# Dilated queries per head with zero rows, value matmuls with the values moving, differential inputs by head pairs

## The chip, the cores and the metric

The kernel runs on one core of a Trainium2 chip. The metric is device time in microseconds (us) from the program's start to its end. The instruction engines are TensorE (matmuls and transposes; PE in the rows, its weight loads PEld), VectorE (DVE), ScalarE (ACT), GpSimd (POOL) and SyncE (SP). SP and POOL also start DMA transfers, each from a queue of its own.

## The reference

One layer of a decoder trunk: 512 tokens, width 1024, float32. A normalised input h goes through one projection `h @ w_in` into four branches and four gates; the branches are RWKV-7, dilated attention, differential attention and a convolution. Their 256-wide outputs go through `w_branch`, are weighted by sigmoid gates, summed and sent through `w_out`; a SwiGLU block follows. The change touches the two attention branches:

```python
# dilated: 3 groups (window, dilation) x 4 heads of 64, softmax over 3 groups at the end
s = einsum('brcqhd,brckhd->brchqk', qb, kb) * 64 ** -0.5      # plus ALiBi bias and mask
lse = logsumexp(s); o = einsum('brchqk,brckhd->brcqhd', exp(s - lse), vb)
out = sum(softmax(stack(lses)) * stack(outs))
...
# differential: 4 heads, each with two maps of 32 columns, values of 64
s = einsum('bqhmd,bkhmd->bhmqk', q_blk, k) * 32 ** -0.5       # plus ALiBi bias and mask
pr = softmax(s); att = pr[:, :, 0] - lam * pr[:, :, 1]
o = einsum('bhqk,bkhd->bqhd', att, vf)                        # then RMS norm per head
```

## The kernel before, in words

**Products.** A weight block comes by DMA from SP's queue into one of two raw buffers (`wload`, line 135). ScalarE casts it to a high half in float32r (line 154), VectorE subtracts for the low half (line 157), each in two pieces; high and low halves have two buffers each. A product of `cm_gemm` (line 194) runs 8 contraction blocks of three 128x512 matmuls (`mm3`, line 188). Its result lies in PSUM under the tag g, two buffers. The gate products (`gates`, line 311: g for the gate, p for the branch projection) and the dilated q, k products are what TensorE has beside the attention work.

**Order.** Within an engine the instructions run in the order that a scheduler fixes at build time from priorities and dependencies, so that attention matmuls stand between the gate products. `place` and `PLACE` (line 26) put single steps behind a named product. TensorE, ScalarE and VectorE each keep one such order, and an instruction that waits holds all behind it.

**Differential attention.** `diff_gemm` (553) makes q and k and spills them to DRAM by POOL's queue. `diff_chain` (573) reads `lam` (row_lam), then loads stacks of 96 rows: high, low, high of q against high, high, low of k, so that one matmul does a three-term product. There are 8 stack entries for 4 heads of two maps; per pair of heads six loads of 256 KB and half of the bias df_b (512 KB). All of these lie in tiles of their own for both pairs, and POOL issues both sets one behind the other (lines 593 to 601). Then, per pair hp, query tile t, head and map: the score dfs (TensorE, line 617, width at least 256 columns), bias and row maximum (VectorE, df_x and df_nm, 620), exponential (ScalarE, 622), the two maps joined (VectorE, 628), transposes dfp (631), a copy pT (ScalarE, 633). The value matmul dfo (638) has the values as the stationary operand, 64 columns, and pT as the moving one, 128 columns:

```python
nc.tensor.matmul(out=o[i * 64:i * 64 + 64, tq], lhsT=X["v"][:, j, h * 64:(h + 1) * 64], rhs=PT[i][:, j, :],
                 start=(j == 0), stop=(j == t))
```

so the two heads of a pair write the two 64-row halves of one PSUM tile (tag o). At the end o is copied to z, transposed back (dfr, four per pair, 645), scaled, normed per head (df_m, and df_r with `pow` on POOL, line 227), transposed (dfy) and split into the branch's y.

**Dilated attention.** `dil_product` (694) makes q and k for a pair of heads and a group. Heads lie in the lower and upper 64 rows of a tile. Group 0 is split into high and low halves (`split_from`: ScalarE casts, VectorE subtracts); groups 1 and 2 are copied with their tokens sorted by residue mod 4. In `dil_chain` (720) the scores dls contract over one head's 64 rows: three float32r matmuls of 256 columns for kind 0 (744), two float32 matmuls of 128 columns for kind 1 (747). Then follow bias, exponential, transposes dlp (753), copies, and value matmuls dlo (763), of the same form as dfo. Kind 1's statistics are exchanged by two small DMAs (774, 776), the weights of both kinds are spread over 64 columns (dl_rb), transposed (dlw, 795) and multiplied onto the outputs. Two biases dl_b of 512 KB (716) come by POOL's queue behind gate02's split.

Of the kernel before, what the change touches and what calls it, by code (L numbers as in the profile page):

```python
# [108 lines left out]
def kern(tc, A):  # L109
    nc = tc.nc  # L110
    W = A["wblk"]
    with ExitStack() as ctx:
# [150 lines left out]
        with ExitStack() as mx:  # L263
            mp = mx.enter_context(tc.tile_pool(name="mix", bufs=1, reuse_waits="tile"))
            with ExitStack() as bx:
# [39 lines left out]
                env = dict(hold=hold, behind=behind, place=place, later=later, after_norm=after_norm, products=products, wx=wx, splits=splits, ups=ups, nc=nc, tc=tc, A=A, vec=vec, HALF=HALF, ps=ps, gps=gps, sps=sps, ops=ops, cm_gemm=cm_gemm, tm_gemm=tm_gemm,  # L305
# [266 lines left out]

def diff_chain(E, pool, X):
# [5 lines left out]
    bias = pool.tile([128, 4, S], F32, name="df_b")  # L579
# [109 lines left out]
def dil_tiles(pool, hp):  # L689
    out = {(n, g): pool.tile([128, S], dt, name=f"dl_{n}{g}{hp}") for n, g, dt in DIL_PARTS}  # L690
    return out


def dil_product(E, hp, nm, g, out):

    p = E["gps"](f"dl{nm}{hp}{g}")
    E["cm_gemm"](p, f"dil_{nm}{hp}{g}")
    if g == 0:
        E["split_from"](p, out[(nm + "0", 0)], out[(nm + "1", 0)])
    else:  # L700
        with E["tc"].high_priority(offset=PRI):
            E["nc"].scalar.copy(out=out[(nm, g)].rearrange("p (r i) -> p r i", r=4), in_=p.rearrange("p (i r) -> p r i", r=4))
# [10 lines left out]
def dil_bias(E, pool, hp):  # L713
    bias = pool.tile([128, 2, 512], F32, name=f"dl_b{hp}")
    with E["tc"].issue_after(E["splits"]["gate02"]):
        E["nc"].gpsimd.dma_start(out=bias, in_=E["A"]["dilb"][:, 2 * hp:2 * hp + 2, :])
    return bias


def dil_chain(E, pool, hp, qk, bias, v, y):  # L720
    nc, ident, sps, pps, ops = E["nc"], E["ident"], E["ops"], E["sps"], E["ups"]
    num, st = [], []
    for kind in range(2):
        o = ops([128, S], f"dlo{hp}{kind}")
        stat = pool.tile([128, NT, 2, 2], F32, name=f"dl_st{hp}{kind}", tag=f"dl_st{kind}", bufs=2)
        for t in range(NT):
# [44 lines left out]
        st.append(stat)

    dS = E["dram"].tile([S, 4], F32, name=f"dl_dS{hp}")
    nc.gpsimd.dma_start(out=dS.rearrange("(i r) s -> i r s", r=4), in_=st[1].rearrange("p r h s -> p r (h s)"))
    sB = pool.tile([128, NT, 2, 2], F32, name=f"dl_sB{hp}", tag="dl_sB", bufs=2)
    nc.gpsimd.dma_start(out=sB.rearrange("p t h s -> p t (h s)"), in_=dS.rearrange("(t p) s -> p t s", p=128))
    w = pool.tile([128, 2, NT, 2], F32, name=f"dl_w{hp}", tag="dl_w", bufs=2)
    d = pool.tile([128, 2, NT, 2], F32, name=f"dl_d{hp}", tag="dl_d", bufs=2)
    both = (st[0], sB)
    nc.vector.tensor_tensor(out=d[:, 0], in0=st[0][:, :, :, 0], in1=sB[:, :, :, 0], op=ALU.min)  # L780
    for k in range(2):
        nc.vector.tensor_tensor(out=w[:, k], in0=d[:, 0], in1=both[k][:, :, :, 0], op=ALU.subtract)
    nc.scalar.activation(out=w, in_=w, func=AF.Exp)
    for k in range(2):
        nc.vector.tensor_tensor(out=d[:, k], in0=w[:, k], in1=both[k][:, :, :, 1], op=ALU.mult)
    nc.vector.tensor_tensor(out=d[:, 0], in0=d[:, 0], in1=d[:, 1], op=ALU.add)
    nc.vector.reciprocal(out=d[:, 0], in_=d[:, 0])
    rb = pool.tile([128, 2, NT, 2, 64], F32, name=f"dl_rb{hp}", tag="dl_rb", bufs=1)
    for k in range(2):
        nc.vector.tensor_tensor(out=w[:, k], in0=w[:, k], in1=d[:, 0], op=ALU.mult)  # L790
        nc.vector.tensor_copy(out=rb[:, k], in_=w[:, k].unsqueeze(3).to_broadcast([128, NT, 2, 64]))

        p = pps([128, S], f"dlw{hp}{k}")
        for t in range(NT):
            tr = nc.tensor.transpose(out=p[:, t * 128:(t + 1) * 128], in_=rb[:, k, t].rearrange("p a b -> p (a b)"), identity=ident)
            E["later"].setdefault(f"dlw{hp}{k}", tr.ins)
        nc.vector.tensor_tensor(out=num[k], in0=num[k], in1=p, op=ALU.mult)
    nc.vector.tensor_tensor(out=num[0], in0=num[0], in1=num[1], op=ALU.add)
    E["split_from"](num[0], y[0][:, hp, :], y[1][:, hp, :])
# [498 lines left out]
```

## Time and profile before

| quantity | value |
|---|---|
| runs | 994.23, 995.0, 996.42 us, median 995.0 |
| profiled execution | 999.86 us, span 997.9 us |
| granted TensorE clock, mean | 0.991 of full speed |
| TensorE / its weight loads | 97% / 81% busy |
| VectorE / ScalarE / GpSimd | 51% / 36% / 8% busy |

The profile shows one execution. Windows give the busy time in a stretch of time, with the granted clock as a share of full speed; a timeline gives single instructions with start and length, and in brackets the idle time in front and what ended it. A timeline row joins neighbours of one form (x2, x8); a float32 matmul leaves two records. The forms are written as rows and columns of the array (128\*64 is half the columns, 64\*128 half the rows), then the moving operand. Differential attention lies between 300 and 431 us, the dilated chains between 400 and 473 us.

### The profile page before, as it was taken

How to read it: one execution, taken by the hardware profiler on the slowest of the kernel's cores; microseconds unless marked ns; L12 is line 12 of the kernel's file. 1: busy time of each engine (PE TensorE's matmuls, PEld its weight loads, DVE VectorE, ACT ScalarE, POOL GpSimd, SP SyncE). 2: the span in 40 equal slices, each digit the busy share in tenths (PEclk: the TensorE clock that was granted, in tenths of full speed). 3: DMA queues.
4: the chain of work that ended last, by engine and by line, in shares of the span. 5: the costliest groups of instructions: out<-in, count | busy, mean ns of one | idle time of the engine just before them, and what ended most of it. 6: DMA issues, size and time to landing. Idle time of an engine off the chain costs nothing.

```text
span 997.9 us, 13474 instructions
## 1 busy us (share of the span) xinstructions
PE 971.5 (97%) x5260; PEld 812.9 (81%) x5260; DVE 508.3 (51%) x1098; ACT 361.2 (36%) x746; POOL 77.0 (8%) x119
## 2 busy tenths in 40 slices
PE   6999999999997999999999999999999999999996
PEld 5887888899985777676888899998888888888885
DVE  4899948346443746544556557634333333322224
ACT  5343613221133635535335446533223232321213
POOL 3000230310140000000000001100000000000003
PEclk9999989999998999999999999999999999999999
DMA  5232533301299122121435235332322323223232
GB/s 189 93 110 85 159 108 104 106 22 44 85 188 236 54 74 64 43 64 44 143 107 181 98 105 170 119 115 85 106 93 98 105 85 105 89 101 102 89 106 84
DMA packets 29775, 103.73 MB, mean 104 GB/s; under 512 B 3600, under 2 KB 3792, under 8 KB 29712
## 3 DMA queue, kind: packets, MB, share of 16 engines
q1 hardware_dynamic: 23472, 87.37, 26.5%
q0 software_dynamic: 6096, 15.24, 6.5%
q8 instruction: 41, 0.67, 0.3%
q10 hardware_dynamic: 144, 0.26, 0.1%
q14 instruction: 22, 0.18, 0.1%
HBM read 97.08 MB, written 5.78 MB: 103 GB/s over the span
## 4 chain that ended last, share of the span: by engine, by line
PE 52%; issue 37%; DVE 4%; DMA 4%; POOL 2%; ACT 1%; SPq 0%; DVEq 0%; POOLq 0%; ACTq 0%
PE g L188 17%; PE p L188 4%; PE dlv L188 3%; PE wo L188 3%; PE dlq L188 2%; PE dlk L188 2%; PE rw_p L997 1%; PE dlo L763 1%; DMA wr_dil_k<-in_wblk_dram 1%; PE cva L188 1%; PE rwr L188 1%; PE rwk L188 1%; PE rwz L188 1%; PE dlp L753 1%; PE rwv L188 1%
## 5 line engine op out<-in xcount | busy, mean ns | idle before, releaser
L188 PE MATMUL g<-h_hi,wh_gate 128*128 128x512 f32 x256 | 101.6, 397 | 0.0
L188 PE MATMUL g<-h_lo,wh_gate 128*128 128x512 f32 x256 | 101.1, 395 | 0.0
L188 PE MATMUL g<-h_hi,wl_gate 128*128 128x512 f32 x256 | 100.9, 394 | 0.0
L188 PE MATMUL fu<-h_lo,wh_fu 128*128 128x512 f32 (+1 forms) x200 | 72.8, 364 | 0.0
L188 PE MATMUL fg<-h_hi,wh_fg 128*128 128x512 f32 (+1 forms) x200 | 72.8, 364 | 0.0
L188 PE MATMUL fu<-h_hi,wh_fu 128*128 128x512 f32 (+1 forms) x200 | 72.7, 363 | 0.0
L188 PE MATMUL fu<-h_hi,wl_fu 128*128 128x512 f32 (+1 forms) x200 | 72.7, 363 | 0.0
L188 PE MATMUL fg<-h_lo,wh_fg 128*128 128x512 f32 (+1 forms) x200 | 72.7, 363 | 0.0
L188 PE MATMUL fg<-h_hi,wl_fg 128*128 128x512 f32 (+1 forms) x200 | 72.7, 363 | 0.0
L157 DVE TENSOR_TENSOR wl_dn<-wr_dn,wh_dn 128x512 fp32r<-128x512 f32 x44 | 28.5, 689 | 85.6 <-ACT wh_dn L154 85.6
L188 PE MATMUL dn<-wl_dn,fh 128*128 128x512 f32 x176 | 68.5, 389 | 0.0
L188 PE MATMUL dn<-wh_dn,fl 128*128 128x512 f32 x176 | 68.5, 389 | 0.0
L188 PE MATMUL dn<-wh_dn,fh 128*128 128x512 f32 x176 | 68.4, 390 | 0.0
L157 DVE TENSOR_TENSOR wl_fg<-wr_fg,wh_fg 128x512 fp32r<-128x512 f32 x46 | 29.7, 688 | 62.2 <-ACT wh_fg L154 62.1
L157 DVE TENSOR_TENSOR wl_gate<-wr_gate,wh_gate 128x640 fp32r<-128x640 f32 x64 | 53.7, 852 | 15.0 <-ACT wh_gate L154 14.9
L154 ACT CAST wh_dn<-wr_dn 128x512 fp32r<-128x512 f32 x44 | 25.1, 619 | 93.2 <-PE dn L188 81.6
L321 ACT ACTIVATE th<-g,hb 128x512 f32<-128x512 f32 x32 | 22.0, 689 | 100.5 <-PE g L188 100.5
L188 PEld LDWEIGHTS g<-h_hi,wh_gate 128*128 128x128 f32 x256 | 48.5, 190 | 10.4 <-issue 0.9
L188 PEld LDWEIGHTS g<-h_lo,wh_gate 128*128 128x128 f32 x256 | 48.5, 190 | 9.8 <-issue 0.3
L188 PEld LDWEIGHTS g<-h_hi,wl_gate 128*128 128x128 f32 x256 | 48.4, 189 | 9.7 <-issue 0.2
L408 DVE TENSOR_TENSOR sg<-fu,sg 128x512 f32<-128x512 f32 (+1 forms) x25 | 15.6, 627 | 79.8 <-PE fu L188 78.6
L154 ACT CAST wh_gate<-wr_gate 128x640 fp32r<-128x640 f32 x64 | 43.9, 725 | 29.2 <-DMA wr_gate<-in_wblk_dram 15.8
(429 smaller groups left out, 2297.0 us busy)
## 6 DMA issues: line engine op xcount, KB each, us to landing
wr_gate<-in_wblk_dram SPq DMA_DIRECT2D x32, 640.0 KB, 3.8
wr_fu<-in_wblk_dram SPq DMA_DIRECT2D x24, 512.0 KB, 3.4
wr_fg<-in_wblk_dram SPq DMA_DIRECT2D x23, 512.0 KB, 3.5
wr_dn<-in_wblk_dram SPq DMA_DIRECT2D x22, 512.0 KB, 3.4
wr_out<-in_wblk_dram SPq DMA_DIRECT2D x14, 512.0 KB, 3.5
wr_dil_v<-in_wblk_dram SPq DMA_DIRECT2D x6, 512.0 KB, 3.5
wr_dil_q<-in_wblk_dram SPq DMA_DIRECT2D x6, 512.0 KB, 3.5
wr_dil_k<-in_wblk_dram SPq DMA_DIRECT2D x6, 512.0 KB, 3.5
```

The source lines that it names most:

```text
L154: nc.scalar.copy(out=hi[:, s], in_=raw[:, s])
L157: sub = nc.vector.tensor_tensor(out=lo[:, s], in0=raw[:, s], in1=hi[:, s].bitcast(F32), op=ALU.subtract)
L188: ins = nc.tensor.matmul(out=ps, lhsT=a[i], rhs=b[j], start=first and i + j == 0, stop=last and i == 1)
L321: nc.scalar.activation(out=th, in_=g, func=AF.Tanh, bias=hb[:, n * 8 + d:n * 8 + d + 1], scale=0.5)
L408: nc.vector.tensor_tensor(out=sg[:, :n], in0=u[:, ts_], in1=sg[:, :n], op=ALU.mult)
L753: nc.tensor.transpose(out=pt[:, b, :], in_=X[:, b * 128:(b + 1) * 128], identity=ident)
L763: nc.tensor.matmul(out=o[i * 64:i * 64 + 64, tq], lhsT=v[:, j, g, h * 64:h * 64 + 64], rhs=PT[i][:, b, :], start=(b == 0), stop=(b == len( ...
L997: nc.tensor.matmul(out=p[:, h, :], lhsT=lhs[:, h, :], rhs=rhs[:, h, :], start=True, stop=True)
```

## The change

Dilated q is kept per head: a tile of 128 rows, 2 heads, 512 tokens, in which the other head's 64 rows are zero. POOL clears these tiles (`memset`, 128x1024), and the q copies write them in two halves of 64 rows. The scores then contract over 128 rows. The value matmuls take pT as the stationary operand and the values, 64 columns, as the moving one; their output has tokens as rows, and all of a tile accumulate behind one `start` (`one_start`). In differential attention o has this layout already, so z's copy and the transposes dfr go; bias and stacks are per pair, with one buffer, so the second pair's loads wait until the first pair's tiles are read. In dilated attention both kinds' statistics are exchanged (four small DMAs for two), the outputs are scaled before the transposes dlw, and a copy and an add join the two kinds. The biases dl_b come behind the first pair's norm (`pows[-2]`) in place of gate02's split.

```diff
+def one_start(E):
+    before = []
+    def accumulate(out, lhsT, rhs, stop):
+        mm = E["nc"].tensor.matmul(out=out, lhsT=lhsT, rhs=rhs, start=not before, stop=stop)
+        if before:
+            E["behind"](mm.ins, before[-1])
+        before.append(mm.ins)
+    return accumulate
...
-    bias = pool.tile([128, 4, S], F32, name="df_b")
-    st = {nm: pool.tile([96, 8, S], F32R, name=f"df_stack{nm}") for nm in "qk"}
-    for hp in range(2):
-        with tc.issue_after(E["splits"]["dil_k02"]) if hp else nullcontext():
-            hs = slice(2 * hp, 2 * hp + 2)
-            for nm, order in (("q", (0, 1, 0)), ("k", (0, 0, 1))):
-                for r, i in enumerate(order):
-                    nc.gpsimd.dma_start(out=st[nm][32 * r:32 * r + 32, 4 * hp:4 * hp + 4], in_=X[nm][i, hp].rearrange("(c d) t -> d c t", d=32))
-            nc.gpsimd.dma_start(out=bias[:, hs], in_=E["A"]["diffb"][:, hs])
     for hp in range(2):
-        o = ops([128, S], f"dfo{hp}")
+        bias = pool.tile([128, 2, S], F32, name=f"df_b{hp}", tag="df_b")
+        nc.gpsimd.dma_start(out=bias, in_=E["A"]["diffb"][:, 2 * hp:2 * hp + 2])
+        st = {nm: pool.tile([96, 4, S], F32R, name=f"df_stack{nm}{hp}", tag=f"df_stack{nm}") for nm in "qk"}
+        for nm, order in (("q", (0, 1, 0)), ("k", (0, 0, 1))):
+            for r, i in enumerate(order):
+                nc.gpsimd.dma_start(out=st[nm][32 * r:32 * r + 32], in_=X[nm][i, hp].rearrange("(c d) t -> d c t", d=32))
+        o = ops([128, NT, 2, 64], f"dfo{hp}")
+        accumulate = one_start(E)
...
-            for j in range(t + 1):
-                for i in range(2):
-                    h = 2 * hp + i
-                    nc.tensor.matmul(out=o[i * 64:i * 64 + 64, tq], lhsT=X["v"][:, j, h * 64:(h + 1) * 64], rhs=PT[i][:, j, :],
-                                     start=(j == 0), stop=(j == t))
+            for i in range(2):
+                h = 2 * hp + i
+                for j in range(t + 1):
+                    accumulate(o[:, t, i, :], PT[i][:, j, :], X["v"][:, j, h * 64:(h + 1) * 64], stop=(i == 1 and j == t == NT - 1))
...
-        nc.scalar.copy(out=z, in_=o)
-        p = pps([128, NT, 2, 64], f"dfr{hp}")
-        for t in range(NT):
-            nc.tensor.transpose(out=p[:, t].rearrange("p a b -> p (a b)"), in_=z[:, t * 128:(t + 1) * 128], identity=ident)
...
+        for t in [out[("q0", 0)], out[("q1", 0)]] if g == 0 else [out[("q", g)]]:
+            nc.gpsimd.memset(t.bitcast(F32) if g == 0 else t, 0.0)
+        for i in range(2):
+            R = slice(i * 64, i * 64 + 64)
+            if g == 0:
+                hi, lo = (out[(f"q{j}", 0)][R, i, :] for j in range(2))
+                nc.scalar.copy(out=hi, in_=p[R])
+                nc.vector.tensor_tensor(out=lo, in0=p[R], in1=hi.bitcast(F32), op=ALU.subtract)
+            else:
+                nc.scalar.copy(out=by4(out[("q", g)][R, i, :]), in_=mod4(p[R]))
...
-    with E["tc"].issue_after(E["splits"]["gate02"]):
+    with E["tc"].issue_after(E["pows"][-2].ins):
...
-                        nc.tensor.matmul(out=s, lhsT=qk[(a, 0)][R, tq], rhs=qk[(b, 0)][R, kk], start=(j == 0), stop=(j == 2))
+                        nc.tensor.matmul(out=s, lhsT=qk[(a, 0)][:, i, tq], rhs=qk[(b, 0)][:, kk], start=(j == 0), stop=(j == 2))
...
-                        nc.tensor.matmul(out=s[:, (g - 1) * 128:g * 128], lhsT=qk[("q", g)][R, tq], rhs=qk[("k", g)][R, tq], start=True, stop=True)
+                        nc.tensor.matmul(out=s[:, (g - 1) * 128:g * 128], lhsT=qk[("q", g)][:, i, tq], rhs=qk[("k", g)][:, tq], start=True, stop=True)
...
-            for b, (g, j) in enumerate(blocks):
-                for i in range(2):
-                    h = 2 * hp + i
-                    nc.tensor.matmul(out=o[i * 64:i * 64 + 64, tq], lhsT=v[:, j, g, h * 64:h * 64 + 64], rhs=PT[i][:, b, :],
-                                     start=(b == 0), stop=(b == len(blocks) - 1))
+            for i in range(2):
+                h = 2 * hp + i
+                for b, (g, j) in enumerate(blocks):
+                    accumulate(o[:, t, i, :], PT[i][:, b, :], v[:, j, g, h * 64:h * 64 + 64], stop=(t == NT - 1 and i == 1 and b == len(blocks) - 1))
```

How the order of instructions moves, first on ScalarE where the first dilated q (dl_q_2584, from the PSUM tile dlq_2592) is cast. Before:

```order
L163 CAST y_hi_2070<-rw_gT 128x512 x2
L163 CAST dl_q_2584<-dlq_2592 128x512
L154 CAST wh_dil_k_2699<-wr_dil_k_2697 128x512
L163 CAST dl_k_2586<-dlk_2627 128x512
L154 CAST wh_dil_k_2699<-wr_dil_k_2697 128x512
L585 ACTIVATE df_ls<-df_ls 128x2
```

Now:

```order
L163 CAST y_hi_2070<-rw_gT 128x512 x2
L719 CAST dl_q_2584<-dlq_2592 64x512
L154 CAST wh_dil_k_2705<-wr_dil_k_2703 128x512
L719 CAST dl_q_2584<-dlq_2592 64x512
L163 CAST dl_k_2586<-dlk_2631 128x512
L154 CAST wh_dil_k_2705<-wr_dil_k_2703 128x512
```

The cast of q has become two of 64 rows, and the second stands behind the first piece of wh_dil_k, the high half of the next weight block.

Next on POOL, where the differential inputs are loaded (32x4x512 is one stack load; df_r is the norm's `pow`). Before:

```order
L129 DMA row_lam<-in_rows_dram 128x128
L600 DMA df_stackq<-df_dq 32x4x512 x3
L600 DMA df_stackk<-df_dk 32x4x512 x3
L601 DMA df_b<-in_diffb_dram 128x1024
L600 DMA df_stackq<-df_dq 32x4x512 x3
L600 DMA df_stackk<-df_dk 32x4x512 x3
L601 DMA df_b<-in_diffb_dram 128x1024
L716 DMA dl_b_3627<-in_dilb_dram 128x1024
L716 DMA dl_b_3629<-in_dilb_dram 128x1024
L227 TENSOR_TENSOR df_r<-df_m,half_neg 128x8 x2
```

Now, from the last two of four memsets on:

```order
L714 MEMSET dl_q_2588 128x1024
L714 MEMSET dl_q_2590 128x1024
L129 DMA row_lam<-in_rows_dram 128x128
L608 DMA df_b_2823<-in_diffb_dram 128x1024
L612 DMA df_stackq_2825<-df_dq 32x4x512 x3
L612 DMA df_stackk_2826<-df_dk 32x4x512 x3
L612 DMA df_stackq_3050<-df_dq 32x4x512 x2
L608 DMA df_b_3048<-in_diffb_dram 128x1024
L612 DMA df_stackq_3050<-df_dq 32x4x512
L612 DMA df_stackk_3051<-df_dk 32x4x512
L227 TENSOR_TENSOR df_r<-df_m,half_neg 128x8
```

Row_lam and the loads stand behind the memsets; the first pair's df_r stands between the second pair's k stacks, and the two dl_b, here below the excerpt, come after them.

Last on TensorE, in the dense stretch of the first dilated pair, from the first score of kind 1 (dls100). Before:

```order
L747 MATMUL dls100_3751<-dl_k10_2589,dl_q10_2588 128x128
L747 MATMUL dls100_3751<-dl_k20_2591,dl_q20_2590 128x128
L747 MATMUL dls110_3762<-dl_k10_2589,dl_q10_2588 128x128
L753 MATMUL dlp012_3709<-ident_64,dl_x012_3702 128x128 x2
L763 MATMUL dlo00_3636<-dl_pT002_3700,dl_v_1693 64x128
L747 MATMUL dls110_3762<-dl_k20_2591,dl_q20_2590 128x128
L753 MATMUL dlp003_3725<-ident_64,dl_x003_3718 128x128 x2
L763 MATMUL dlo00_3636<-dl_pT012_3712,dl_v_1693 64x128
L763 MATMUL dlo00_3636<-dl_pT002_3700,dl_v_1693 64x128
L763 MATMUL dlo00_3636<-dl_pT012_3712,dl_v_1693 64x128
```

Now:

```order
L769 MATMUL dls100_3749<-dl_k10_2589,dl_q10_2588 128x128
L769 MATMUL dls100_3749<-dl_k20_2591,dl_q20_2590 128x128
L775 MATMUL dlp012_3708<-ident_64,dl_x012_3701 128x128 x2
L769 MATMUL dls110_3760<-dl_k10_2589,dl_q10_2588 128x128
L775 MATMUL dlp003_3724<-ident_64,dl_x003_3717 128x128 x2
L769 MATMUL dls110_3760<-dl_k20_2591,dl_q20_2590 128x128
L769 MATMUL dls101_3775<-dl_k10_2589,dl_q10_2588 128x128
L578 MATMUL dlo00_3636<-dl_v_1693,dl_pT012_3711 128x64 x2
L775 MATMUL dlp013_3736<-ident_64,dl_x013_3729 128x128 x2
L578 MATMUL dlo00_3636<-dl_v_1693,dl_pT003_3727 128x64 x2
```

The score and value rows that stood one by one between transposes as 64-row or 64-column forms are now whole-array rows; two of a head's value matmuls follow each other.

## Rows read from the trace of the kernel before

**Rows 1.** The page, part 1: busy us, share of span, instructions

```profile
PE 971.5 (97%) x5260; PEld 812.9 (81%) x5260; DVE 508.3 (51%) x1098; ACT 361.2 (36%) x746; POOL 77.0 (8%) x119
```

**Rows 2.** Groups by shape, TensorE: count | busy us, mean ns | idle before

```profile
L617 PE MATMUL dfs<-df_stackk,df_stackq 96*128 96x256 f32 x16 | 4.4, 327 | 5.4 <-DVE df_nm L620 5.4
...
L617 PE MATMUL dfs<-df_stackk,df_stackq 96*128 96x384 f32 x8 | 2.9, 365 | 1.1 <-DVE df_nm L620 1.1
```

**Rows 3.** Windows: length, busy (x records) by engine, clock, DMA share, GB/s

```profile
300.00:325.00 25.00, 19.62 (x83) 14.82 (x81) 10.06 (x35) 9.67 (x28) 1.46 (x3) 0.86 0.93 229
378.00:431.00 53.00, 53.00 (x324) 37.32 (x323) 30.37 (x94) 30.84 (x86) 2.25 (x2) 1.00 0.13 41
```

**Rows 4.** Timeline of TensorE (start, length, what): dlq's first and last product

```profile
287.24 0.39 PE L188 MATMUL dlq<-h_hi,wh_dil_q 128*128 128x512 f32 x1
...
292.45 0.39 PE L188 MATMUL dlq<-h_hi,wl_dil_q 128*128 128x512 f32 x1
```

**Rows 5.** Timeline of TensorE: one value matmul and seven between products

```profile
394.95 0.40 PE L188 MATMUL dlq<-h_lo,wh_dil_q 128*128 128x512 f32 x1
395.28 0.43 PE L638 MATMUL dfo<-df_pT,df_v 128*64 128x128 f32 x2
...
395.98 0.40 PE L188 MATMUL dlq<-h_hi,wh_dil_q 128*128 128x512 f32 x1
...
398.05 0.39 PE L188 MATMUL dlq<-h_lo,wh_dil_q 128*128 128x512 f32 x1
398.37 1.09 PE L638 MATMUL dfo<-df_pT,df_v 128*64 128x128 f32 x14
...
399.72 0.40 PE L188 MATMUL dlq<-h_hi,wh_dil_q 128*128 128x512 f32 x1
```

**Rows 6.** Timeline of TensorE: whole-array f32 matmuls of the RWKV part

```profile
214.52 1.00 PE L1090 MATMUL rw_pW<-rw_X,rw_K 128*128 128x64 f32 x8
215.33 0.36 PE L188 MATMUL dlv<-wh_dil_v,h_hi 128*128 128x256 f32 x1
215.53 0.28 PE L188 MATMUL dlv<-wl_dil_v,h_hi 128*128 128x256 f32 x1
```

**Rows 7.** Windows of line 188 alone: length, busy (x records), clock, DMA

```profile
322.00:350.00 28.00, 21.85 (x77) 1.00 0.15 48
378.00:431.00 53.00, 29.23 (x100) 1.00 0.13 41
449.00:473.00 24.00, 5.83 (x19) 1.00 0.13 46
```

**Rows 8.** Timeline of TensorE: first and last change of form, 322 to 473

```profile
322.79 0.43 PE L638 MATMUL dfo<-df_pT,df_v 128*64 128x128 f32 x2
...
471.95 0.50 PE L188 MATMUL g<-h_hi,wh_gate 128*128 128x512 f32 x1
```

**Rows 9.** Timeline of ScalarE, with idle time before and its releaser

```profile
314.96 0.72 ACT L154 CAST wh_gate<-wr_gate 128x640 fp32r<-128x640 f32 x1 [5.65 <-DMA wr_gate<-in_wblk_dram]
```

**Rows 10.** Chain of waits, 300 to 320: start, length, what

```profile
304.26 10.60 DMA wr_gate<-in_wblk_dram
```

**Rows 11.** DMA table, 275 to 325: packets, MB, share; issues, us to landing

```profile
q0 software_dynamic: 2624, 6.36, 64.7%
...
df_stackk<-df_dk POOLq DMA_DIRECT2D x6, 256.0 KB, 15.1
```

**Rows 12.** Windows, columns as in group 3: behind two waits

```profile
316.80:322.00 5.20, 5.19 (x16) 3.68 (x17) 3.61 (x16) 2.84 (x13) 0.00 (x0) 0.59 0.51 172
122.50:130.00 7.50, 7.48 (x35) 6.91 (x36) 4.95 (x11) 1.29 (x3) 0.54 (x1) 0.54 0.73 239
```

**Rows 13.** Groups by shape, POOL

```profile
L979 POOL MEMSET rw_K<- 128x1024 f32 x2 | 1.9, 964 | 29.5 <-DVE rw_KL L963 29.5
```

**Rows 14.** Timeline of VectorE: y's lower halves

```profile
283.27 1.28 DVE L164 TENSOR_TENSOR y_lo<-rw_gT,y_hi 128x512 fp32r<-128x512 f32 x2
```

**Rows 15.** Timeline of ScalarE: wh_dil_k's cast

```profile
287.25 0.62 ACT L154 CAST wh_dil_k<-wr_dil_k 128x512 fp32r<-128x512 f32 x1 [3.43 <-issue]
```

More of the change, by code (lines that the diff above doesn't have):

```diff
@@ L304, in kern @@
                 after_norm = pows[-1].ins
-                env = dict(hold=hold, behind=behind, place=place, later=later, after_norm=after_norm, products=products, wx=wx, splits=splits, ups=ups, nc=nc, tc=tc, A=A, vec=vec, HALF=HALF, ps=ps, gps=gps, sps=sps, ops=ops, cm_gemm=cm_gemm, tm_gemm=tm_gemm,
+                env = dict(hold=hold, pows=pows, behind=behind, place=place, later=later, after_norm=after_norm, products=products, wx=wx, splits=splits, ups=ups, nc=nc, tc=tc, A=A, vec=vec, HALF=HALF, ps=ps, gps=gps, sps=sps, ops=ops, cm_gemm=cm_gemm, tm_gemm=tm_gemm,
                            wload=wload, V=V, row_bc=row_bc, rstd_of=rstd_of, ident=ident, cp=cp, mp=mp, split_from=split_from,
@@ L616, in diff_chain @@
                     w = max(n, 256)
-                    nc.tensor.matmul(out=s[:, :w], lhsT=st["q"][:, 2 * h + m, tq], rhs=st["k"][:, 2 * h + m, :w], start=True, stop=True)
+                    nc.tensor.matmul(out=s[:, :w], lhsT=st["q"][:, 2 * i + m, tq], rhs=st["k"][:, 2 * i + m, :w], start=True, stop=True)
                     xx = pool.tile([128, S], F32, name=f"df_x{t}{h}{m}", tag="df_x", bufs=4)
                     nm = pool.tile([128, 1], F32, name=f"df_nm{t}{h}{m}", tag="df_nm", bufs=4)
-                    nc.vector.tensor_tensor_reduce(out=xx[:, :n], in0=s[:, :n], in1=bias[:, h, S - n:], scale=-cs, scalar=BIG * 4,
+                    nc.vector.tensor_tensor_reduce(out=xx[:, :n], in0=s[:, :n], in1=bias[:, i, S - n:], scale=-cs, scalar=BIG * 4,
                                                    op0=ALU.add, op1=ALU.min, accum_out=nm)
@@ L689, in dil_tiles @@
 def dil_tiles(pool, hp):
-    out = {(n, g): pool.tile([128, S], dt, name=f"dl_{n}{g}{hp}") for n, g, dt in DIL_PARTS}
-    return out
+    return {(n, g): pool.tile([128, 2, S] if n[0] == "q" else [128, S], dt, name=f"dl_{n}{g}{hp}") for n, g, dt in DIL_PARTS}
 def dil_product(E, hp, nm, g, out):
@@ L697, in dil_product @@
     E["cm_gemm"](p, f"dil_{nm}{hp}{g}")
[L698 to L702, printed above, removed]
+    nc = E["nc"]
+    mod4 = lambda a: a.rearrange("p (i r) -> p r i", r=4)
+    by4 = lambda a: a.rearrange("p (r i) -> p r i", r=4)
+    if nm == "k" and g == 0:
+        E["split_from"](p, out[("k0", 0)], out[("k1", 0)])
+        return
+    with E["tc"].high_priority(offset=PRI):
+        if nm == "k":
+            nc.scalar.copy(out=by4(out[("k", g)]), in_=mod4(p))
+            return
+        for t in [out[("q0", 0)], out[("q1", 0)]] if g == 0 else [out[("q", g)]]:
[8 more added lines that the diff above has]
+                nc.scalar.copy(out=by4(out[("q", g)][R, i, :]), in_=mod4(p[R]))
 def dil_qk(E, pool, hp):
@@ L721, in dil_chain @@
     nc, ident, sps, pps, ops = E["nc"], E["ident"], E["ops"], E["sps"], E["ups"]
-    num, st = [], []
+    num = []
+    st = pool.tile([128, 2, 2, NT, 2, 2], F32, name=f"dl_st{hp}", tag="dl_st", bufs=2)
     for kind in range(2):
-        o = ops([128, S], f"dlo{hp}{kind}")
-        stat = pool.tile([128, NT, 2, 2], F32, name=f"dl_st{hp}{kind}", tag=f"dl_st{kind}", bufs=2)
+        o = ops([128, NT, 2, 64], f"dlo{hp}{kind}")
+        accumulate = one_start(E)
+        stat = st[:, kind, kind]
         for t in range(NT):
@@ L770, in dil_chain @@
-        num.append(z)
[L771 to L778, printed above, removed]
@@ L779, in dil_chain @@
-    both = (st[0], sB)
-    nc.vector.tensor_tensor(out=d[:, 0], in0=st[0][:, :, :, 0], in1=sB[:, :, :, 0], op=ALU.min)
+            for i in range(2):
+                h = 2 * hp + i
+                for b, (g, j) in enumerate(blocks):
+                    accumulate(o[:, t, i, :], PT[i][:, b, :], v[:, j, g, h * 64:h * 64 + 64], stop=(t == NT - 1 and i == 1 and b == len(blocks) - 1))
+        z = pool.tile([128, NT, 2, 64], F32, name=f"dl_num{hp}{kind}", tag=f"dl_num{kind}", bufs=1)
+        nc.scalar.copy(out=z, in_=o)
@@ new lines, in dil_chain @@
+        num.append(z)
+    orders = ("(t p) s -> p t s", "(p t) s -> p t s")
+    for kind in range(2):
+        dS = E["dram"].tile([S, 4], F32, name=f"dl_dS{hp}{kind}")
+        nc.gpsimd.dma_start(out=dS.rearrange(orders[kind], t=NT), in_=st[:, kind, kind].rearrange("p t h s -> p t (h s)"))
+        nc.gpsimd.dma_start(out=st[:, 1 - kind, kind].rearrange("p t h s -> p t (h s)"), in_=dS.rearrange(orders[1 - kind], t=NT))
+    w = pool.tile([128, 2, 2, NT, 2], F32, name=f"dl_w{hp}", tag="dl_w", bufs=2)
@@ L781, in dil_chain @@
+    d = pool.tile([128, 2, 2, NT, 2], F32, name=f"dl_d{hp}", tag="dl_d", bufs=2)
+    nc.vector.tensor_tensor(out=d[:, :, 0], in0=st[:, :, 0, :, :, 0], in1=st[:, :, 1, :, :, 0], op=ALU.min)
     for k in range(2):
-        nc.vector.tensor_tensor(out=w[:, k], in0=d[:, 0], in1=both[k][:, :, :, 0], op=ALU.subtract)
+        nc.vector.tensor_tensor(out=w[:, :, k], in0=d[:, :, 0], in1=st[:, :, k, :, :, 0], op=ALU.subtract)
     nc.scalar.activation(out=w, in_=w, func=AF.Exp)
     for k in range(2):
-        nc.vector.tensor_tensor(out=d[:, k], in0=w[:, k], in1=both[k][:, :, :, 1], op=ALU.mult)
@@ L793, in dil_chain @@
         p = pps([128, S], f"dlw{hp}{k}")
         for t in range(NT):
[L795 to L799, printed above, removed]
+            tr = nc.tensor.transpose(out=p[:, t * 128:(t + 1) * 128], in_=num[k][:, t].rearrange("p a b -> p (a b)"), identity=ident)
@@ L803, in rwkv_gemm @@
+            E["later"].setdefault(f"dlw{hp}{k}", []).append(tr.ins)
+        turned.append(p)
+    out = pool.tile([128, S], F32, name=f"dl_out{hp}", tag="dl_out", bufs=1)
+    nc.scalar.copy(out=out, in_=turned[0])
+    nc.vector.tensor_tensor(out=out.rearrange("p (i r) -> p i r", r=4), in0=out.rearrange("p (i r) -> p i r", r=4),
+                            in1=turned[1].rearrange("p (r i) -> p i r", r=4), op=ALU.add)
+    E["split_from"](out, y[0][:, hp, :], y[1][:, hp, :])
 def rwkv_gemm(E, pool):
```

19 lines of the change are left out of this document (7 added, 12 removed).

## The prediction, made before the changed kernel was run

> **What bounds the kernel now.** I read the engine totals first [rows 1]: TensorE is busy 97% of the span, VectorE 51%, ScalarE 36%. So time is saved only where TensorE gets less to do, or where one of its few waits goes. Its costly groups come second [rows 2]: the differential scores (dfs) are the only ones in the attention part with idle time of size before them, 5.4 and 1.1 us, all of it on VectorE. Third come the windows [rows 3]: in 300 to 325 TensorE works 19.62 of 25 us at a mean clock of 0.86, with the DMA engines busy at 0.93; in 378 to 431 it is full and the DMAs are at 0.13. So the change touches two places of different kinds: a stall near 310 beside full DMAs, and full stretches in which only the price of each matmul form counts.
>
> **Price of the forms.** The 24 products of one dlq start between 287.24 and 292.45, one every 0.227 us [rows 4]. One value matmul (its two records are the "x2") stands between two products: from 394.95 to 395.98 are 1.03 us, less two products 0.58. Seven in a row: from 398.05 to 399.72 are 1.67, less two products 1.22 [rows 5]. The difference gives (1.22 - 0.58)/6 = 0.107 us for one matmul, and the 0.47 that remain are paid for going into the half-array form and out again: **0.23 us for a change of form**. The kind that the new value matmul will be (whole array, f32, 128 stationary and 64 moving columns) exists in the RWKV part: eight records, four matmuls, take from 214.52 to 215.33, and the step behind them is 0.08 longer than the 0.12 of its kind, so 0.89 in all [rows 6]: **0.222 us each**, 0.111 a record, with nothing to see of a change of form. I take 0.11 for a transpose too, one record of the same kind. A value matmul by itself thus doubles, 0.107 to 0.222; what can pay for that is the changes of form that go.
>
> **The full stretches.** Three windows hold nearly all of the attention matmuls. From each length I take the work that stays: products, counted in [rows 7], at 0.227, transposes at 0.11, differential scores by their columns (0.114, 0.170, 0.227). The rest is the price of value matmuls, dilated scores and changes of form. By the loops a differential pair has 20 value matmuls, a dilated pair 30 and 40 score matmuls, 16 in f32 and 24 in f32r.
> 322 to 350: 77 products 17.5, scores 2.7, 23 transposes 2.5, rest 5.3, for 19 value matmuls of the first pair. After: 19 x 0.222 = 4.2. Gain 1.1, and four transposes of z that go, 0.4: 1.5.
> 378 to 431: 100 products 22.7, 62 transposes 6.8, scores 1.3, rest 22.2, for 50 value matmuls and 40 dilated scores. After: 50 x 0.222 + 16 x 0.222 (nearest rows again [rows 6]) + 24 x 0.12 (the 256-column step of [rows 6]) = 17.5. Gain 4.7, and four transposes: 5.1.
> 449 to 473: 19 products 4.3, 30 transposes 3.3, rest 16.4, for 30 value matmuls and 40 scores. After: 6.7 + 3.6 + 2.9 = 13.2. Gain 3.2.
> Sum **9.8 us**. Cross-check: by my count of the timeline these windows hold 104 changes between half-array and whole-array rows, the first at 322.79, the last at 471.95 [rows 8]. At 0.23 they cost 23.9; the added work is 99 value matmuls x 0.115 + 32 f32 scores x 0.11 = 14.9; with the 0.9 of eight transposes the gain is 9.9. The two agree.
>
> A rule speaks against the change. The Trainium skill, "TensorEngine Tiling (Array Packing)", section Performance Considerations, says that a dimension of 64 should be given to half-array tiles, for up to twice the rate. For a matmul by itself the trace agrees (0.107 against 0.222); by this rule alone the stretches would get 14 us longer. The same page of the Trainium skill, section Key Properties, says that a change of tiling mode drains TensorE, and the 0.23 us of [rows 5] agree.
>
> **The stall at 308 to 322.** Two scores wait 5.4 us for VectorE [rows 2]. VectorE stood behind the lower half of wh_gate, that behind ScalarE's cast, and that waited 5.65 us for the DMA of wr_gate [rows 9]; in the chain of waits this transfer takes 10.60 us from 304.26 [rows 10]. The DMA table of 275 to 325 tells why: POOL's queue, with 12 stack loads, two df_b and two dl_b, moves 6.36 MB and holds 64.7% of the engines' time [rows 11] beside SP's weights. Behind the wait TensorE works at a mean clock of 0.59 from 316.8 to 322 [rows 12], which loses 5.2 x 0.41 = 2.1. Together 7.5. Now only the first pair's share goes in here, six stack loads and a bias, 2.1 MB; 3.1 MB stand behind the first pair's last score or its norm, and SP's queue keeps its order. wr_gate is then asked for when almost nothing else moves. Between 0 and 7.5 I take 7.5. The third wait, 1.1 us [rows 2], sits on a second-pair score that now comes later: 1.1 gone.
>
> **What it adds.** (a) Four POOL memsets of 128x1024, 0.96 us each [rows 13], stand ahead of row_lam and of all differential loads. They wait, as the copies do, for y's lower half, which ends at 284.55 [rows 14]; so the loads go in from 288.4, and even at the 15.1 us of now [rows 11] the first land at 303.5, ahead of wr_gate's request and of the scores behind it. Hidden, by some 5 us. (b) The q copies come in 64-row halves, and on ScalarE the second stands behind the cast of wh_dil_k, which starts only as dlk's last product ends, at 287.25 [rows 15]. PSUM's buffer of dlq is then free only after that cast, the copy, and VectorE's two subtractions, about 0.5 each: 289.2, and the next dlq, which started at 287.24 [rows 4], waits: **2.0 us** (ends: 0.6 if VectorE's come at once, 3 if a memset is late too). The clock may fall behind it: behind a wait that ends at 122.5 it was 0.54 until 130 [rows 12]; that would be another 3.4 us (7.5 x 0.46). This wait follows long full work, so I take it as an even chance and leave it out of the sum. (c) In the full stretches TensorE gets faster, while ScalarE and VectorE keep 30 of 53 us of work [rows 3], so the chain score, exponential, transpose, copy, value matmul gets tighter: 2 us (0 to 4). (d) The second pair's loads wait for the last score of the first; by the order 87 products, 20 us, then stand ahead of its first score. At 0.15 of DMA there [rows 7] I take no cost. (e) The added statistics DMAs and the scaling ahead of dlw's transposes lie beside gate products: nothing (up to 1).
>
> **Sum.** -9.8 - 7.5 - 1.1 + 2.0 + 2.0 = -14.4. The profiled execution took 999.86 us, 4.9 above the median of 995.0. The sum is laid on the median: 980.6, rounded **981 us**. If those 4.9 lie in the stall, the median runs have that much less to gain.
>
> **Rivals.**
> 1. The stall's gain is smaller, or spent again: half clock behind the wait at 287 (+3.4), or the 4.9 just named, or both: 984 to 989, about 987. For it: both waits of [rows 12] were followed by about half the clock.
> 2. The second pair's loads come late. Its tiles are single buffers; POOL stands in a wait for TensorE and VectorE, and the last k stacks are behind the norm's df_r. If q stacks and then k stacks take 15.1 us each, one behind the other, 30, the cover of 20 is short by 10; with a partial overlap by 6.6, and half the clock behind that costs 3.4: 991. Against it: the idle DMAs there.
> 3. Slower: half-array pairs run side by side and a change of form costs little where changes are dense. Then 14.9 is added, less 0.9, with -8.6 for the stalls and +4 for the new waits: 1004. It decides where a change costs under 14/104 = 0.13 us; [rows 5] show 0.23, and the window sum bears it out. It is what the Trainium skill's page on tiling, named above, would give by its Performance Considerations.
> 4. More gain: the chain (c) costs nothing and the wait at 287 is 0.6: 977.
> That the change does not do what it says is excluded by the order: every value matmul stands there as 128x64.
>
> **Chances.** Forecast (978.5 to 984) 0.52; rival 1 0.22; rival 2 0.08; rival 3 0.06; rival 4 (972 to 978.5) 0.12. A measurement of this kernel tells 0.2% (2 us) from no change. Faster by more: all but rival 3 and a little of 2, 0.91; same 0.03; slower 0.06. The range, 973 to 990, leaves out rival 3, most of rival 2 and the far ends of 1 and 4.
>
> **What would show it.** Value matmuls of 128x64 at 0.22 us each without 0.2 us around them; no wait above 1 us at dfs, clock 1.00 from 300 to 325, wr_gate landing in some 4 us; a wait of about 2 us of dlq near 287. Wrong would be: a wait of several us at the second pair's first score, a rest above 20 us in the stretch of 53, or a half clock behind a new wait.

## The result, and the profile after

The changed kernel takes **982.39 us** in the median (981.67 to 986.45), the kernel before, measured beside it, 995.71: ratio 0.9872, 95% interval 0.9838 to 0.9906, so it is 1.3% faster. Forecast were 981 and a range of 973 to 990. The profiled execution took 982.15 us, span 980.2.

The engine totals, the list of TensorE's waits and the windows of the changed kernel, to be held against [rows 1], [rows 2] and [rows 3]:

```profile
PE 957.4 (98%) x5252; PEld 818.3 (83%) x5252; DVE 510.6 (52%) x1096; ACT 365.5 (37%) x752; POOL 86.9 (9%) x131
```

```profile
PE hnp L251 <- DVE hnj L238: 8.1, 2, 7.8
PE dlq L188 <- DVE dl_q L720: 2.0, 1, 2.0
PE rw_pA L955 <- DVE rw_bW L932: 1.3, 1, 1.3
```

```profile
300.00:325.00 25.00, 25.00 (x127) 20.59 (x126) 17.13 (x57) 15.56 (x43) 1.08 (x2) 1.00 0.41 113
380.00:417.00 37.00, 36.94 (x251) 32.82 (x251) 21.53 (x62) 20.92 (x60) 6.34 (x7) 1.00 0.14 44
435.00:457.00 22.00, 21.98 (x169) 20.23 (x168) 10.68 (x42) 13.59 (x45) 3.14 (x5) 1.00 0.17 51
```

The waits at dfs are gone, 300 to 325 is full at full clock with the DMAs at 0.41 in place of 0.93, and one wait is new: dlq for VectorE, 2.0 us. The last two of these windows cover the dilated chains: TensorE idles 0.08 us in them. In the DMA table of 275 to 325, the weights before, then POOL's queue [rows 11] and the weights now:

```profile
wr_gate<-in_wblk_dram SPq DMA_DIRECT2D x4, 640.0 KB, 9.1
```

```profile
q0 software_dynamic: 1603, 3.68, 38.5%
...
wr_gate<-in_wblk_dram SPq DMA_DIRECT2D x5, 640.0 KB, 4.5
```

wr_gate lands in 4.5 us in the median where it took 9.1, and 10.60 for the one in the chain of waits [rows 10]. The new wait, on ScalarE and then on TensorE:

```profile
282.06 0.58 ACT L719 CAST dl_q<-dlq 64x512 fp32r<-64x512 f32 x1 [2.33 <-POOL dl_q L714]
283.60 0.62 ACT L154 CAST wh_dil_k<-wr_dil_k 128x512 fp32r<-128x512 f32 x1 [0.96 <-PE dlk L188]
284.24 0.58 ACT L719 CAST dl_q<-dlq 64x512 fp32r<-64x512 f32 x1
```

```profile
285.81 0.47 PE L188 MATMUL dlq<-h_hi,wh_dil_q 128*128 128x512 f32 x1 [2.03 <-DVE dl_q L720]
```

The second half of q's cast stands behind wh_dil_k's cast, which waits for the last dlk product, as (b) of the prediction had it. The first half waits for POOL's memset, which (b) did not have; it is done before that product ends, so it does not set the 2.03. The clock stayed at 1.00 behind these 2.03 us.

**Where the spans differ.** The two profiles' spans differ by 17.7 us; about 3.0 of that is no work of the change: from 122 to 130, before any changed instruction, the clock was at half in the profile before and not in this one, behind the same wait of 1.3 us. That wait ends at 122.52 before and at 121.91 now, 0.61 apart; the first dlq product is 3.61 apart. Of the twelve profiles below, one (e7) has the half clock there too.

The window 125 to 130, first before, then after:

```profile
125.00:130.00 5.00, 5.00 (x23) 4.55 (x23) 2.45 (x8) 0.59 (x1) 0.54 (x1) 0.51 0.66 213
```

```profile
125.00:130.00 5.00, 5.00 (x35) 4.23 (x34) 3.53 (x13) 0.59 (x1) 0.54 (x1) 1.00 0.57 185
```

So the changed part is read between products that both kernels have. From the first dlq product (275.61 before, 272.00 after) to the p product behind the second dilated chain (475.49 and 457.30) the gain is 199.88 - 185.30 = 14.6 us; the sum of the prediction was 14.4. The medians differ by 13.3.

### The profile page after: what moved, and what is told of

The parts are those of the page before. It is cut to its first block, busy times and chain, and to the rows that moved or that the text cites. A ratio compares the mean times of both kernels' runs of the same rounds, so it can differ in the third digit from the quotient of the medians.

```text
span 980.2 us, 13497 instructions
## 1 busy us (share of the span) xinstructions
PE 957.4 (98%) x5252; PEld 818.3 (83%) x5252; DVE 510.6 (52%) x1096; ACT 365.5 (37%) x752; POOL 86.9 (9%) x131
## 4 chain that ended last, share of the span: by engine, by line
PE 55%; issue 37%; DVE 3%; POOL 2%; DMA 1%; ACT 1%; SPq 0%; DVEq 0%; POOLq 0%; ACTq 0%
PE g L188 18%; PE p L188 4%; PE dlv L188 3%; PE dlk L188 3%; PE wo L188 3%; PE dlq L188 3%; PE rw_p L1017 1%; PE dlo L578 1%; PE cva L188 1%; PE rwr L188 1%; PE rwk L188 1%; PE rwz L188 1%; PE rwv L188 1%; PE dfq L188 1%; PE cvb L188 1%
## 5 line engine op out<-in xcount | busy, mean ns | idle before, releaser
L154 ACT CAST wh_fu<-wr_fu 128x512 fp32r<-128x512 f32 x48 | 27.5, 620 | 72.0 <-PE fu L188 71.4
```

The costliest lines, as they stand in the source:

```text
L154: nc.scalar.copy(out=hi[:, s], in_=raw[:, s])
```

## The experiments

**One part alone: the loads (e1).** On the kernel before:

```diff
-    bias = pool.tile([128, 4, S], F32, name="df_b")
...
+        bias = pool.tile([128, 2, S], F32, name=f"df_b{hp}", tag="df_b")
+        st = {nm: pool.tile([96, 4, S], F32R, name=f"df_stack{nm}{hp}", tag=f"df_stack{nm}") for nm in "qk"}
...
-    with E["tc"].issue_after(E["splits"]["gate02"]):
+    with E["tc"].issue_after(E["pows"][-2].ins):
```

> The kernel before with one part of the change alone: bias and stacks of the differential inputs per pair in single buffers, dl_b behind the first pair's norm. Half-array scores and value matmuls stay. My theory (the stall at 308 to 322 comes from the second pair's transfers and dl_b sharing the DMAs with wr_gate): the stall and the wait at 351 go, 7.5 + 1.1 = 8.6 us, so about 987 against 995.7; no idle time before dfs, clock 1.00 in 300 to 325, no wait of dlq at 287. Rival (the stall comes from the order of instructions on ScalarE and VectorE, and went because the changed order is another): 994 to 997, wr_gate lands sooner but the wait stays.

Measured: 987.58 us against 995.24, ratio 0.9929 (0.9909 to 0.9950). Its window and its DMA table of 275 to 325:

```profile
300.00:325.00 25.00, 25.00 (x129) 18.68 (x128) 18.41 (x61) 16.04 (x46) 1.77 (x4) 1.00 0.42 123
```

```profile
q0 software_dynamic: 1584, 3.61, 39.1%
...
wr_gate<-in_wblk_dram SPq DMA_DIRECT2D x5, 640.0 KB, 3.8
```

ScalarE's cast of wh_gate that waited 5.65 us for the DMA [rows 9] now waits for a product alone:

```profile
305.13 0.73 ACT L154 CAST wh_gate<-wr_gate 128x640 fp32r<-128x640 f32 x1 [3.60 <-PE dlk L188]
```

Between the products at 309 and 378 it gains 8.7 us (forecast 8.6), behind that nothing: both dilated chains are as long as before. The rival of another order falls: from the first dlq product to 337 us of the kernel before, behind the stall, ScalarE, VectorE and TensorE work on the same tiles in the same order in both traces. What differs is POOL's queue. So the transfers were the cause; no matmul changed its form here.

**The matmul forms, one at a time (e2, e3, e7).** e2 is e1 with the zero rows, that is, whole-array scores and half-array value matmuls. e3 is the changed kernel with 64-row scores, that is, whole-array value matmuls alone:

```diff
-                        nc.tensor.matmul(out=s, lhsT=qk[(a, 0)][:, i, tq], rhs=qk[(b, 0)][:, kk], start=(j == 0), stop=(j == 2))
+                        nc.tensor.matmul(out=s, lhsT=qk[(a, 0)][R, tq], rhs=qk[(b, 0)][R, kk], start=(j == 0), stop=(j == 2))
```

> e1 and the zero rows: q per head with zero rows, whole-array scores; value matmuls stay half-array. By the order 82 changes of form are left of 120. My theory (a change costs 0.20 to 0.23 us): 38 x 0.2 = 7.6 less, 32 f32 scores dearer by 0.11 = 3.6 more, the wait of dlq at 287 2.0 more: about 2 us under e1, 985. Rival (half-array matmuls are dear by themselves, changes of form cost little; then the gains of scores and values add up to the whole): e2 and e3 lie together as far below e1 as the changed kernel does, some 5 us for the two.

> The changed kernel with the scores as before: q without zero rows, 64-row scores, no memsets; value matmuls swapped, loads per pair. By the order 64 changes of form are left of 120. My theory: 56 x 0.2 = 11.2 less than e1, 99 value matmuls dearer by 0.115 = 11.4 more, the eight transposes of z 0.9 less: within 1 us of e1, about 986.5; so the two parts together give some 3 us under e1 and the whole change 5 or more, since only both together remove the last 26 changes. No wait of dlq at 287. Rival (values cost by themselves): e3 is well under e1, and e2's and e3's distances from e1 add up to that of the changed kernel.

> e3 once more, for a profile in which the second dilated chain is not at half clock: 987 to 988.5; the two dilated chains together no shorter than in e1.

Measured: e2 988.24, e3 988.13, e1 beside them 987.58; e7 989.64 (the kernel before beside it 994.82, beside the others 995.24). Each part alone gives nothing that can be told from e1; of e2 I had expected 2 us, and e7 lies above the 987 to 988.5 that I had named. The table has, per kernel, the length of three stretches between the same products, and the changes of form that I counted in each. Of the 59 and the 45, seven each lie between the two half-array forms (64 rows and 64 columns), all others between half-array and whole-array rows (stretch 1: first gate product beside dfs to the last gate product before the dilated chains; 2: from there to the fifth dlk; 3: sixth dlk to the p product behind the second chain):

| kernel | 1: us, changes | 2: us, changes | 3: us, changes |
|---|---|---|---|
| before | 69.3, 16 | 53.9, 59 | 31.2, 45 |
| e1, loads | 60.5, 16 | 54.0, 59 | 31.2, 45 |
| e2, loads and scores | 61.2, 16 | 52.9, 42 | 29.0, 24 |
| e7, loads and values | 59.8, 0 | 53.0, 30 | 32.4, 34 |
| changed kernel | 59.9, 0 | 50.0, 0 | 28.0, 0 |

The ends of stretch 3, in the changed kernel and in e7:

```profile
429.30 0.39 PE L188 MATMUL dlk<-h_hi,wh_dil_k 128*128 128x512 f32 x1
...
457.30 0.39 PE L188 MATMUL p<-y_hi,wh_gate 128*128 128x512 f32 x1
```

```profile
433.36 0.39 PE L188 MATMUL dlk<-h_hi,wh_dil_k 128*128 128x512 f32 x1
...
465.74 0.39 PE L188 MATMUL p<-y_hi,wh_gate 128*128 128x512 f32 x1
```

In stretches 2 and 3 together the scores alone gain 3.3 us on e1 and the values alone lose 0.3; both together gain 7.2. Parts that priced their own matmuls would add up. What is left over, 4.2 us, fits the changes of form that go only when nothing half-array is left (104 in these two stretches, 38 by the scores, 40 by the values, 26 by both together; at the 0.18 us that d1 to d3 give below, 4.7). That takes 0.18 for every change; d1 to d3 measure it between 64 columns and the whole array alone, and no run has the price of the others by itself. Over the whole kernel e2 gives most of its 3.3 back: dlq waits 2.0 us as in the changed kernel, and stretch 1 is 0.7 longer.

**The loads early again (e4).** The changed kernel, with two buffers for q stacks and bias, and both dl_b behind gate02's split again:

> The changed kernel with the second pair's q stacks, its bias and both dl_b (2.3 of 3.1 MB) asked for right behind the first pair's loads again. My theory: wr_gate lands late again, ScalarE and VectorE wait for it, dfs waits 2 to 6 us near 310 and the clock may fall: 985 to 990 against 982.4. Rival (the stall went because of the new order of instructions, not of the transfers): within 1 us of 982.4.

Measured: 986.06 us (984.75 to 987.09). The time is in the expected range, the mechanism only in part. wr_gate's transfer in the chain of waits takes 8.82 us again, and ScalarE waits for it, but sooner; of TensorE's waits at dfs there are two:

```profile
299.29 8.82 DMA wr_gate<-in_wblk_dram
```

```profile
305.17 0.73 ACT L154 CAST wh_gate<-wr_gate 128x640 fp32r<-128x640 f32 x1 [6.63 <-DMA wr_gate<-in_wblk_dram]
```

```profile
PE dfs L640 <- DVE df_nm L643: 1.6, 2, 1.2
```

One of them, 0.45 us, lies at 308.85; the other, 1.16, at 341.00, is on the second pair. POOL's last early issue ended at 297.6 here, at 307.0 before; why the scores wait so little here, by the 2.3 in place of 3.1 MB or by the sooner end, was not told apart. So e4 shows wr_gate delayed by the early loads, and not the stall; its span is 2.2 us longer than the changed kernel's (982.4 and 980.2), of which these waits are 1.6. That e1 takes the stall away, with the engines' order as it was, settles the cause.

**The price of a form by itself (d1 to d5).** 64 matmuls, whose results nothing reads, among the products of the gate that comes last in the changed kernel (eight output blocks of 24 products). In d1 and d5 one stands behind each three products, in d2 to d4 eight in a row in the middle of each output block, behind the fourth contraction block:

```diff
+ mm = nc.tensor.matmul(out=du[0][:64, :128], lhsT=ident[:, :64], rhs=ident, start=True, stop=True)      # d1, d2
+ mm = nc.tensor.matmul(out=du[0][half, :128], lhsT=ident[:, :64], rhs=ident, start=True, stop=True)     # d3
+ mm = nc.tensor.matmul(out=du[0][:, :64], lhsT=ident, rhs=ident[:, :64], start=True, stop=True)         # d4, d5
```

> The changed kernel with 64 added matmuls of no use among the gate products of the last gate, one behind each three products, in the old value form (64 stationary columns of the identity, 128 moving, f32). My theory: each costs 0.107 and two changes of form, 0.47, so 0.58 each, 37 us in all: 1019. Rival (half-array matmuls cost, the change does not): as the blocks of d2, 0.11 each, 7 us.

> The same 64 added matmuls in 8 blocks of 8. My theory: 64 x 0.107 + 8 x 0.47 = 10.6 us more than the changed kernel, 993. Rival (the price is that of the single matmul): the same as d1.

> As d2, 64 added matmuls in 8 blocks of 8, but each second one into the upper 64 rows of the output, as the value matmuls of two heads stood before. d2 took 15.5 us more than the changed kernel, 1.94 a block, which by a form change of 0.23 leaves 0.18 to 0.20 for one matmul. Theory A (two halves work side by side, so neighbours of different halves cost 0.107 and neighbours in one half 0.20): 8 x (8 x 0.107 + 0.4) = 10 us over the changed kernel, about 994. Theory B (0.20 is the price of any half-array matmul, and 0.107 was read wrongly): as d2, 1000.

> As d2, but in the new value form: whole array, 128 stationary and 64 moving columns. 64 x 0.222 = 14.2 us over the changed kernel, 998.5. If whole-array matmuls were dearer than in the RWKV part: above 1000; if a pair of whole-array ones overlapped: under 995.

> As d1, one added matmul behind each three products, but in the new value form, so without a change of form. My theory: 14.2 us over the changed kernel as in d4, 998.5, against 35 of d1, so that two changes of form are 35.3 less 64 x 0.20 = 22.5 us, 0.35 for the two. Rival (any matmul of another shape between products pays the same): as d1, 1019.

Measured: 1019.62, 999.79, 994.55, 997.99 and 999.96 us, against 984.28 of the changed kernel beside d1 and d2 (e6, below); the kernel before took 995.83 beside these and 994.82 beside d3 to d5. d3 was the least steady, 991.92 to 1001.27. Timelines of TensorE, of d1 and d5 two added matmuls one after the other, three products between them:

```profile
520.70 0.43 PE L216 MATMUL du<-ident 128*64 128x128 f32 x2
...
521.95 0.43 PE L216 MATMUL du<-ident 128*64 128x128 f32 x2
```

```profile
509.62 0.33 PE L216 MATMUL du<-ident 128*128 128x64 f32 x2
...
510.54 0.33 PE L216 MATMUL du<-ident 128*128 128x64 f32 x2
```

Less three products, 0.68, a half-array matmul alone costs 0.57 and a whole-array one 0.24. Of d2, d3 and d4 a block of eight, with the product ahead and the second one behind:

```profile
518.64 0.39 PE L190 MATMUL g<-h_hi,wl_gate 128*128 128x512 f32 x1
518.96 1.96 PE L216 MATMUL du<-ident 128*64 128x128 f32 x16
...
521.19 0.40 PE L190 MATMUL g<-h_lo,wh_gate 128*128 128x512 f32 x1
```

```profile
509.60 0.39 PE L190 MATMUL g<-h_hi,wl_gate 128*128 128x512 f32 x1
509.92 1.09 PE L217 MATMUL du<-ident 128*64 128x128 f32 x16
...
511.28 0.40 PE L190 MATMUL g<-h_lo,wh_gate 128*128 128x512 f32 x1
```

```profile
511.52 0.40 PE L190 MATMUL g<-h_hi,wl_gate 128*128 128x512 f32 x1
511.75 1.90 PE L216 MATMUL du<-ident 128*128 128x64 f32 x16
...
513.77 0.39 PE L190 MATMUL g<-h_lo,wh_gate 128*128 128x512 f32 x1
```

Less two products, 0.45, a block costs 2.10, 1.23 and 1.80. With s for a half-array matmul alone or beside others of its own half, a for one whose neighbours are in the other half, c for going in and out: s + c = 0.57, 8s + c = 2.10, 8a + c = 1.23, so s = 0.22, a = 0.11, c = 0.36, **0.18 a change**. The rows from which I had read the price agree [rows 5]: one gave 0.58 (s + c = 0.58), seven gave 1.22 (s + 6a + c = 1.24, if three pairs overlap and the seventh is taken as one alone). A whole-array one is 1.80/8 = 0.225 in a row. d2 fell outside both of its expectations (15.5 us more than e6, where 10.6 or 35 were named), and d3 settled it.

**The wait of dlq (e5, e6).** The changed kernel with both casts ahead of the subtractions, and only the zero halves cleared; e6 is the changed kernel again.

```diff
-                nc.scalar.copy(out=hi, in_=p[R])
-                nc.vector.tensor_tensor(out=lo, in0=p[R], in1=hi.bitcast(F32), op=ALU.subtract)
+                nc.scalar.copy(out=out[("q0", 0)][R, i, :], in_=p[R])
...
+            for i in range(2):
...
+                nc.vector.tensor_tensor(out=lo, in0=p[R], in1=hi.bitcast(F32), op=ALU.subtract)
```

> The changed kernel with dlq's two casts written ahead of the two subtractions, so that on ScalarE both stand ahead of wh_dil_k's cast, and with only the zero halves of the q tiles cleared (64x512 twice in place of 128x1024). My theory (dlq01 waited 2.0 us because the second cast stood behind wh_dil_k's cast): the wait falls to 0 to 0.6 us, 1.4 to 2.0 us less than the changed kernel run beside it. Rival (the wait is POOL's memset, which starts only at the end of y's lower half): the wait stays above 1 us and the time within 1 us.

> The changed kernel unchanged, on the same chip as e5: 982.4, within 2 us; dlq waits 2.0 us at 286. It gives the distance of e5 in one call.

Measured: e5 981.24 us (980.33 to 983.37), e6 984.28 (982.58 to 984.38), four runs each; e5 to before 0.9854 (0.9831 to 0.9878). Both casts now stand ahead, and the wait of TensorE is gone from the list:

```profile
282.94 1.18 ACT L721 CAST dl_q<-dlq 64x512 fp32r<-64x512 f32 x2 [1.32 <-DVE y_lo L164]
285.50 0.62 ACT L154 CAST wh_dil_k<-wr_dil_k 128x512 fp32r<-128x512 f32 x1 [1.38 <-PE dlk L188]
```

e5 has the lowest median of the study; its interval overlaps that of e6 (0.9857 to 0.9898). Its 3.0 us under e6 are more than the 2.0 of the wait; one measurement tells 2 us, so only the wait's 2.0 is claimed. Two things were edited at once, and the traces tell them apart in the main: POOL's clearing did not get shorter (eight memsets take 4.49 us where four took 3.63), and in the changed kernel the second cast starts at 284.24, as wh_dil_k's cast ends, 2.2 us behind the memset that released the first. So the order of the casts made the 2.0. With the smaller memsets the casts no longer wait for POOL; what that gave by itself was not measured.

## Why the prediction was right, and where it was not

| term | forecast | measured |
|---|---|---|
| stall at 308 to 322 and wait at 351 | -7.5 - 1.1 = -8.6 | -8.7 (e1, stretch 1) |
| full stretches | -9.8 | -7.8 with the next row |
| tighter chains | +2.0 | 0.1 of idle time |
| dlq at 287 | +2.0 | +2.03 |

- **The stall** was right in cause and size, by e1 (the 7.5 and the 1.1 were not measured apart). What it came from, a queue of loads that shares the engines with the weights, was in the DMA table and the chain of waits.
- **The stretches and (c)** came out right in their sum by luck. They gave 0.7 in stretch 1 (changed kernel 9.4 of gain, e1 8.7), where 1.5 were forecast, and 7.1 in the chains (85.1 to 78.0 us), where 8.3 were forecast: 7.8, which is the 9.8 less the 2.0 of (c). But TensorE idles 0.1 us in the chains, so (c) cost nothing, and the 9.8 was 2.0 too much. The step that was off is the rest, which was replaced whole by prices of the new forms. Worked out for stretches 2 and 3 as the forecast did for its windows, the rest of the changed kernel is 19.2 and 13.8 us, 33.0, where 17.5 and 13.2 were forecast; 20 in the first of them was named as a sign of being wrong. (Before it is 22.7 and 17.0 in these stretches; the forecast had 22.2 and 16.4, since two of its 100 and two of its 19 products begin ahead of their window.) The price of the value matmuls is not the reason: from the start of a row to the start of the next the 80 take 17.1 us, 0.213 each, below the 0.222. The f32 scores take 7.7 and the f32r scores 6.4 us, where 7.1 and 5.8 were taken; the 150 products take 36.8 us, 0.245 each, where 0.227 gives 34.1, since the first one behind other matmuls takes longer:

```profile
450.78 0.48 PE L188 MATMUL g<-h_lo,wh_gate 128*128 128x512 f32 x1
451.10 0.40 PE L188 MATMUL g<-h_hi,wl_gate 128*128 128x512 f32 x1
451.33 0.65 PE L578 MATMUL dlo<-dl_v,dl_pT 128*128 128x64 f32 x4
```

  The first of these takes 0.32 us to the next start, the second 0.23. How a step divides between neighbours is not certain from starts alone. d4 against d5, 0.225 in a row and 0.24 alone, gives 0.5 us for the 33 places in these stretches at which products end and other matmuls begin; why the steps between whole-array forms cost the remaining 1.8 is open.
- **The price of a change of form** was read as 0.23 and is 0.18. The step that failed was to fit one and seven value matmuls with one price: the single one costs 0.22, the seven mostly 0.11, since they alternate between two halves. So what the prediction says of a matmul by itself, 0.107 against 0.222, does not hold: by itself it costs as much as a whole-array one. The cross-check of 9.9 us had changes too dear and scattered value matmuls too cheap (0.107 where one stands alone), two errors of opposite sign; it also left out the 14 changes between the two half-array forms. That it agreed with the 9.8 was luck.
- **The wait of dlq** was right to 0.1 us in size, place and order of engines. Half the clock behind it, an even chance, did not come.
- **Rival 2** did not come either: nothing waits at the second pair's first score. **Rival 3** (halves side by side) is right as a mechanism, as d3 shows, and the 0.107 had it in already; it loses because a change costs 0.18, above the 0.13 from which it would decide. The Trainium skill, "TensorEngine Tiling (Array Packing)", section Key Properties, says that different tiles can execute matmuls in parallel; d2 against d3 agrees, 0.22 and 0.11.

## What to carry to other kernels

By these prices half-array matmuls pay where many stand in a row and alternate between halves; scattered one by one among whole-array work each costs 0.57 us here, two changes of form among it, where a whole-array one costs 0.24. So count the changes of form that are left before converting one kind alone: here 82 of 120 stayed with the scores converted and 64 with the values, and each part alone measured as no change (the scores' part lost 2.0 us of its 3.3 to the wait of dlq, which e5's order of casts removes). A load that nobody waits for yet can still be the one to delay: look which transfers share the DMA engines with the weights that are needed next, and ask for the early ones as late as their cover allows.

## What the runs showed of the hardware that I had not expected

Eight half-array matmuls in one half cost 0.22 us each, as much as whole-array ones, and 0.11 when they alternate between halves. And the clock fell in a stretch without a wait that the profile shows: in e3's profile TensorE is busy and at half clock from 452 to about 466, in the second dilated chain:

```profile
448.00:452.00 4.00, 3.93 (x29) 2.90 (x28) 1.64 (x7) 3.22 (x11) 0.00 (x0) 0.99 0.02 2
452.00:456.00 4.00, 4.00 (x18) 3.54 (x18) 0.86 (x3) 0.93 (x4) 0.00 (x0) 0.50 0.00 0
```

That execution took 993.69 us, the other six of e3 987.39 to 989.77. e7, the same kernel, kept its clock there, and its stretch 3 is 32.4 us long, against 38.5 in e3. Why it fell is open.
